# Output projections of a two-layer trunk: first layer's weight sums added by GpSimd, and the second product's operands in the freed input tiles

## The chip, the core and the metric

The kernel runs on one core of a Trainium2 chip. The time is the device time of one execution in microseconds. Engines work side by side: TensorE (PE, with its weight loads as PEld), VectorE (DVE), ScalarE (ACT), GpSimd (POOL), and SyncE (SP), which here issues nearly all DMAs. Each engine works its own instructions off in a fixed order and waits where an operand isn't there. The granted clock (PEclk) is the clock of TensorE as a share of 2.4 GHz; 0.50 is 1.2 GHz.

## The reference

```python
for i in range(DEPTH):                      # two layers, T = 1024 tokens, D = 1024
    hid = _rmsnorm(x, norm_w[i])
    if i % 2 == 0: x = x + _gated_deltanet(hid, ...)   # layer 0
    else:          x = x + _mamba2(hid, ...)           # layer 1
return _rmsnorm(x, final_norm_w)
# each mixer: project hid, convolve, gates, a chunked scan over tokens giving y (T x 2048),
# a gated norm of y, and last the output projection:
#   return y @ w_out                        # (1024 x 2048) times (2048 x 1024), float32
# layer 0, in each chunk of 64 tokens: a unit lower triangular solve with a_mat
```

All in float32. A float32 product is made here of three products of operands split in a high and a low part (hi x hi, hi x lo, lo x hi).

## The kernel before, in words

Both layers have the same course. The normalised hidden rows lie transposed in SBUF in tiles of `apool` (tags a0 to a3, two buffers each of 128 x 4 x 512). Eight groups of heads follow each other. In layer 0, while group g is scanned over its chunks (`scan`), the triangular inverse of group g+1 (`inverse`) and its projections run between, handed out slot by slot in the loop at L909. `inverse` stores nte to a DRAM tile xd (L615), reads it back in another layout into X (L618), writes ones on X's diagonal with a GpSimd memset (L619), and solves row by row on VectorE (L630). The scan carries a state S, written by VectorE (L791, L794) and used by TensorE (L771). A finished chunk is normalised (L820 to L825, two small GpSimd instructions per chunk), turned by TensorE (L66) and stored to DRAM as y, `y0d` or `y1d` (L836).

The output projection (`out_proj`, L346) halves y and w_out in both directions and makes the result in seven products of half size instead of eight. The products' weights are, in order, x00, s1, s2, x01, s3, s4, x11, where x are blocks of w_out and s sums of them: s1 = x10 + x11, s2 = s1 + x00, s3 = x00 + x10, s4 = s2 + x01. Their other operands are blocks of y or differences of such: one running tile Tt of differences for products 1, 2 and 6 (L370, L373), and one difference on GpSimd for product 4 (L365). Products are counted from 0 in this text. Each is 8 k-steps of 12 matmuls 128x512 (4 PSUM banks times three, L387 to L389) and a k-step loads a block of weights (L378) and of y (L357), splits each (`split`: a ScalarE cast at L86, a VectorE subtraction at L87), and goes. Products alternate between PSUM banks ps_proj and ps_pt (even) and ps_tr and ps_sc (odd). The scan uses ps_tr and ps_sc.

The sums lie in DRAM. `weight_sums` (L321) makes them with 44 GpSimd-issued DMAs per layer, 16 copies (L338) and 28 that add to what stands there (L340), of 512 KB; the loops take one per slot during the scan. Product 0 (`early`) runs in the last slots of the last group. Products 1 to 6 (`rest`) begin after the scan: they take a new pool `nrm`, which lies where the scan's pool lay and opens when everything of that has ended. In it are the residual rows `xrow` (L416), Tt, u, and the rings of split operands from product 2 on; product 1 splits into `apool` tiles (`big_ring`, a0 to a3), whose hidden rows are no longer needed. `d0` reads product 0's banks out.

What order the engines get is decided ahead by a scheduler that simulates a timeline; the program's order is its input. DMAs marked `keep_in_program_order` stay in theirs.

## Time and profile before

| | us |
|---|---|
| median of 3 runs (2013.79 to 2020.08) | 2018.72 |
| profiled execution | 2022.02 |
| its span | 2020.3 |
| TensorE busy | 1886.5 |
| VectorE busy | 1402.6 |
| ScalarE busy | 1081.1 |
| GpSimd busy | 576.1 |

The busy times are those of the profiled execution, and the span is that of its instructions. GpSimd's busy time leaves out the DMAs that it issues. TensorE's share is an average over the stages: a hole in it counts in full, and work of the other engines counts only where TensorE waits for it.

### The profile page before, as it was taken

To read this page: it belongs to the slowest core of one execution; us is meant where nothing else is said; L and a number is where in the kernel's file an instruction comes from. 1 tells how busy PE (TensorE), PEld (TensorE's weight loads), DVE (VectorE), ACT (ScalarE), POOL (GpSimd) and SP (SyncE) were. 2 spreads that over 40 slices of the span, in tenths; PEclk is the share of its full clock that TensorE was granted. 3 is DMA by queue.
4 is the path that set the end of the run, shared out by engine and by line. 5 is a ranking of instruction groups with operands and counts; after the bars stand their busy time and mean duration, and the time that the engine had idled before them with its cause. 6 is when DMAs were issued, how large, how long until landed. Compare 5 with 4: busy or idle time off the path is not lost. (4 is left out here: it accounts for less than half of the span.)

```text
span 2020.3 us, 36051 instructions
## 1 busy us (share of the span) xinstructions
PE 1886.5 (93%) x12782; PEld 1615.4 (80%) x12782; DVE 1402.6 (69%) x3011; ACT 1081.1 (54%) x2933; POOL 576.1 (29%) x962
## 2 busy tenths in 40 slices
PE   7996989898998989899799999999999999998897
PEld 5775878787887878788588788888888888887786
DVE  5795767676768676765488777666576666666677
ACT  5634656466565646565444565555445455554343
POOL 1112122223222211110324133424343342432253
PEclk9997999899999989999899999999999999999999
DMA  4444354625444532334566245455464443244864
GB/s 142 112 95 87 88 125 100 128 75 141 94 119 85 115 71 75 86 100 136 186 220 216 80 140 130 111 127 111 123 131 120 115 98 87 83 128 128 266 227 151
DMA packets 260087, 249.98 MB, mean 124 GB/s; under 512 B 67345, under 2 KB 182722, under 8 KB 259906
## 3 DMA queue, kind: packets, MB, share of 16 engines
q1 hardware_dynamic: 240066, 201.54, 34.3%
q0 software_dynamic: 19840, 46.14, 12.1%
q8 instruction: 100, 1.64, 0.3%
q14 instruction: 81, 0.66, 0.1%
HBM read 218.06 MB, written 75.69 MB: 145 GB/s over the span
## 5 line engine op out<-in xcount | busy, mean ns | idle before, releaser
L165 PE MATMUL ps_proj<-hid_h,wh 128*128 128x512 f32 x1024 | 411.8, 402 | 0.8 <-ACT gtmp L268 0.5
L166 PE MATMUL ps_proj<-hid_l,wh 128*128 128x512 f32 x1024 | 405.4, 396 | 0.0
L167 PE MATMUL ps_proj<-hid_h,wl 128*128 128x512 f32 x1024 | 405.1, 396 | 0.0
L227 PE MATMUL ps_proj<-zh,hid_h 128*128 128x256 f32 x1024 | 304.4, 297 | 4.0 <-DVE z L234 2.7
L229 PE MATMUL ps_proj<-zh,hid_l 128*128 128x256 f32 x1024 | 299.6, 293 | 0.0
L228 PE MATMUL ps_proj<-zl,hid_h 128*128 128x256 f32 x1024 | 299.0, 292 | 0.0
L165 PEld LDWEIGHTS ps_proj<-hid_h,wh 128*128 128x128 f32 x1024 | 193.1, 189 | 40.7 <-ACT gtmp L268 0.8
L167 PEld LDWEIGHTS ps_proj<-hid_h,wl 128*128 128x128 f32 x1024 | 192.8, 188 | 40.6
L166 PEld LDWEIGHTS ps_proj<-hid_l,wh 128*128 128x128 f32 x1024 | 193.0, 188 | 36.2
L227 PEld LDWEIGHTS ps_proj<-zh,hid_h 128*128 128x128 f32 x1024 | 200.8, 196 | 8.6 <-DVE z L234 3.3
L228 PEld LDWEIGHTS ps_proj<-zl,hid_h 128*128 128x128 f32 x1024 | 200.4, 196 | 3.0
L229 PEld LDWEIGHTS ps_proj<-zh,hid_l 128*128 128x128 f32 x1024 | 200.1, 195 | 0.4
L204 DVE SCALAR_TENSOR_TENSOR acc<-raw,cw_ssd,acc 128x512 f32<-128x512 f32 x192 | 160.5, 836 | 43.3 <-ACT acc L202 40.0
L204 DVE SCALAR_TENSOR_TENSOR acc<-raw,cw_gdn,acc 128x512 f32<-128x512 f32 x192 | 145.1, 757 | 21.5 <-ACT acc L200 20.2
L317 POOL TENSOR_SCALAR_AFFINE_SELECT gcrow<-gcrow 128x512 f32<-128x512 f32 x128 | 95.4, 754 | 187.3 <-DMA gcrow<-gcr_g 126.4
L821 POOL TENSOR_SCALAR so<-so,cq 128x2 f32<-128x2 f32 x64 | 27.3, 427 | 420.2 <-ACT yn L820 420.2
L87 DVE TENSOR_TENSOR wl<-wr,wh 128x512 fp32r<-128x512 f32 x128 | 89.6, 701 | 79.0 <-ACT wh L86 77.5
L630 DVE TENSOR_TENSOR tm<-Dt,X 128x2 f32<-128x2 f32 (+30 forms) x248 | 86.9, 350 | 75.6 <-POOL X L619 68.0
L184 ACT ACTIVATE th<-acc 128x512 f32<-128x512 f32 x128 | 80.2, 627 | 93.6 <-DVE acc L204 93.4
L86 ACT CAST wh<-wr 128x512 fp32r<-128x512 f32 x128 | 78.8, 617 | 75.9 <-PE ps_proj L166 64.4
L197 ACT COPY raw<-ps_proj 128x512 f32<-128x512 f32 x128 | 74.6, 582 | 77.8 <-PE ps_proj L167 73.6
L1010 ACT ACTIVATE lt<-gcrow,ldt_s 128x128 f32<-128x128 f32 x256 | 82.0, 391 | 40.5 <-POOL t L1015 18.0
(308 smaller groups left out, 4441.8 us busy)
## 6 DMA issues: line engine op xcount, KB each, us to landing
wr<-in_gdn_w_in_dram SPq DMA_DIRECT2D x96, 256.0 KB, 3.1
wr<-in_ssd_w_in_dram SPq DMA_DIRECT2D x96, 256.0 KB, 2.9
wo_gs<-in_gdn_w_out_dram POOLq DMA_DIRECT2D x44, 512.0 KB, 6.4
wo_ss<-in_ssd_w_out_dram POOLq DMA_DIRECT2D x44, 512.0 KB, 6.7
yr<-y0d SPq DMA_DIRECT2D x72, 256.0 KB, 3.6
yr<-y1d SPq DMA_DIRECT2D x72, 256.0 KB, 3.5
gcrow<-gcr_g SPq DMA_DIRECT2D x64, 256.0 KB, 3.7
gcrow<-gcr_s SPq DMA_DIRECT2D x64, 256.0 KB, 4.0
```

What stands on the lines that cost most here:

```text
L87: nc.vector.tensor_tensor(out=lo, in0=src, in1=hi.bitcast(F32), op=ALU.subtract)
L165: nc.tensor.matmul(pt[0:nco], hi[:, j, 0:nco], xh[:, j, :], start=first, stop=False)
L166: nc.tensor.matmul(pt[0:nco], hi[:, j, 0:nco], xl[:, j, :], start=False, stop=False)
L167: nc.tensor.matmul(pt[0:nco], lo[:, j, 0:nco], xh[:, j, :], start=False, stop=last)
L184: nc.scalar.activation(th, src, AF.Tanh, scale=0.5)
L204: nc.vector.scalar_tensor_tensor(out=acc, in0=raw[:, k:k + 512], scalar=cw[:, k * 32 + ti:k * 32 + ti + 1], in1=acc, op0=ALU.mult, op1=ALU ...
L227: nc.tensor.matmul(pt, xh, zh[:, k, :], start=k == 0, stop=False)
L228: nc.tensor.matmul(pt, xh, zl[:, k, :], start=False, stop=False)
L229: nc.tensor.matmul(pt, xl, zh[:, k, :], start=False, stop=k == KT - 1)
L317: nc.gpsimd.affine_select(out=t, in_=t, pattern=[[0, 4], [1, P]], compare_op=ALU.is_ge, fill=-1e30, base=0, channel_multiplier=-1)
L630: nc.vector.tensor_tensor(out=tv, in0=Dt[:, r0:, s:], in1=X[:, s:s + 1, s:].to_broadcast([P, nr, nj]), op=ALU.mult)
L1010: nc.scalar.activation(lt[:, h, :], rows[h][:, n % 4, :], AF.Exp, bias=ldt[:, h0 + h, n:n + 1])
```

## The change

For layer 0 (`made` false) no sums are made in DRAM. Products 1, 2, 4 and 5 load blocks of w_out and GpSimd adds them in SBUF (`w_form`): s1 into tiles W1 (two `apool` tiles a1), on which s2 and s4 go on adding; s3 in place. That is 32 additions 128x512 and 16 more weight loads. In layer 1 the DMAs stay. Product 1's differences go to N1 (two `apool` tiles a0) in both layers, and its split operands to a2 and a3 alone. In layer 0 the differences of products 1 and 4 are made by VectorE, in layer 1 by GpSimd as before. Loading the residual rows and reading out product 0 move behind the third k-step of product 1, two more fetches behind the fifth. Layer 0's allocation of the next hidden tiles moves from product 1 to product 5. The early product's steps are spread 2, 2, 1, 1 over the last slots, one behind the flush, the rest at the end.

```diff
-    def out_proj(yd, forms, resid):
+    def out_proj(yd, X, made, resid):
...
+        N1, W1 = [], []
...
             if i == 4:
                 a, b = load_y(1, 1, j), load_y(0, 1, j, "raw")
-                nc.gpsimd.tensor_tensor(out=a, in0=a, in1=b, op=ALU.subtract)
+                (nc.gpsimd if made else nc.vector).tensor_tensor(out=a, in0=a, in1=b, op=ALU.subtract)
                 return a
-            d = Tt[:, j, :]
             if i == 1:
-                a, b = load_y(0, 0, j), load_y(0, 1, j, "raw")
-                nc.gpsimd.tensor_tensor(out=d, in0=a, in1=b, op=ALU.subtract)
+                a, b, d = load_y(0, 0, j), load_y(0, 1, j, "raw"), N1[j // 4][:, j % 4, :]
+                (nc.gpsimd if made else nc.vector).tensor_tensor(out=d, in0=a, in1=b, op=ALU.subtract)
             else:
-                a = load_y(*{2: (1, 1), 6: (1, 0)}[i], j)
-                nc.vector.scalar_tensor_tensor(out=d, in0=d, scalar=-1.0, in1=a, op0=ALU.mult, op1=ALU.subtract)
+                a, d = load_y(*{2: (1, 1), 6: (1, 0)}[i], j), Tt[:, j, :]
+                nc.vector.scalar_tensor_tensor(out=d, in0=N1[j // 4][:, j % 4, :] if i == 2 else d, scalar=-1.0, in1=a,
+                                               op0=ALU.mult, op1=ALU.subtract)
             return d
 
+        ring_at = [0]
+
+        def load_x(f, j):
+            raw = wring.tile([P, 512], F32, tag=("wr", "wh", "wl")[ring_at[0] % 3], name="wr", bufs=3)
+            ring_at[0] += 1
+            nc.sync.dma_start(raw, X[f][j * P:(j + 1) * P, :])
+            return raw
+
+        def w_form(f, j):
+            if made or f[0] == "x":
+                return load_x(f, j)
+            add = lambda d, a, b: nc.gpsimd.tensor_tensor(out=d, in0=a, in1=b, op=ALU.add)
+            if f == "s3":
+                a, b = load_x("x00", j), load_x("x10", j)
+                add(a, a, b)
+                return a
+            d = W1[j // 4][:, j % 4, :]
+            if f == "s1":
+                add(d, load_x("x10", j), load_x("x11", j))
+            else:
+                add(d, d, load_x({"s2": "x00", "s4": "x01"}[f], j))
+            return d
+
         def pieces(i, j, ring, Tt):
-            raw = wring.tile([P, 512], F32, tag=("wr", "wh", "wl")[j % 3], name="wr", bufs=3)
-            nc.sync.dma_start(raw, forms[wf[i]][j * P:(j + 1) * P, :])
+            raw = w_form(wf[i], j)
...
-        def big_ring(j):
-            a = apool.tile([P, 4, 512], F32R, tag=("a0", "a1", "a2", "a3")[j % 4], name="wy", bufs=2)
-            return [a[:, q, :] for q in range(4)]
+        def in_a(tags):
+            def ring(j):
+                a = apool.tile([P, 4, 512], F32R, tag=tags[j % len(tags)], name="wy", bufs=2)
+                return [a[:, q, :] for q in range(4)]
+            return ring
         banks0 = []
         def early():
             banks0.extend(U())
-            yield from product(0, banks0, big_ring)
+            yield from product(0, banks0, in_a(("a0", "a1", "a2", "a3")))
         def rest(npool, nw, on_rows, before_last=lambda: None):
             rows = {t: [npool.tile([P, D], F32, tag="xr", name="xrow", bufs=NT) for _ in range(4)] for t in range(2)}
             Tt = npool.tile([P, 8, 512], F32, tag="T", name="Tt", bufs=1)
             u = npool.tile([P, 4, 512], F32, tag="u", name="u", bufs=1)
+            N1.extend(apool.tile([P, 4, 512], F32, tag="a0", name="N1", bufs=2) for _ in range(2))
+            if not made:
+                W1.extend(apool.tile([P, 4, 512], F32, tag="a1", name="W1", bufs=2) for _ in range(2))
             half = lambda t, p, c: rows[t][p][:, c * 512:(c + 1) * 512]
             def fetch(t, c):
...
-            fetch(0, 0)
-            for p in range(4):
-                nc.scalar.copy(u[:, p, :], banks0[p])
-                put(0, p, 0, banks0[p], ALU.add)
+            def d0():
+                for p in range(4):
+                    nc.scalar.copy(u[:, p, :], banks0[p])
+                    put(0, p, 0, banks0[p], ALU.add)
...
             for i, done in ((1, d1), (2, d2), (3, d3), (4, d4), (5, d5)):
                 banks = V() if i % 2 else U()
-                for j, _ in enumerate(product(i, banks, big_ring if i == 1 else ring, Tt)):
-                    if j == 3 and i == 1:
+                for j, _ in enumerate(product(i, banks, in_a(("a2", "a3")) if i == 1 else ring, Tt)):
+                    if (i, j) == (1, 2):
+                        fetch(0, 0)
+                        d0()
+                    if (i, j) == (1, 4):
                         fetch(1, 0)
                         fetch(1, 1)
-                    if j == 3 and i == 3:
+                    if (i, j) == (3, 3):
                         fetch(0, 1)
-                if i == 1:
+                if i == 5:
                     before_last()
                 for p in range(4):
                     done(p, banks[p])
...
-    wo0, steps0 = weight_sums(gw_out, "g")
-    early0, rest0 = out_proj(yd0, wo0, lambda n: x[n * P:(n + 1) * P, :])
-    early1, rest1 = out_proj(yd1, wo1, lambda n: x1d[n])
+    wo0 = {f"x{c}{k}": gw_out[k * 1024:(k + 1) * 1024, c * 512:(c + 1) * 512] for c in range(2) for k in range(2)}
+    early0, rest0 = out_proj(yd0, wo0, False, lambda n: x[n * P:(n + 1) * P, :])
+    early1, rest1 = out_proj(yd1, wo1, True, lambda n: x1d[n])
...
             S = scan(g)
             for slot in range(8):
-                next(steps0, None)
                 if g == 7 and slot > 3:
                     next(early0)
-                    next(early0)
+                    if slot < 6:
+                        next(early0)
                 for c in "SIJ":
...
             if g < 6:
                 for _ in k_products(g + 2):
                     pass
+            elif g == 7:
+                next(early0)
             next(S, None)
             if g < 7:
                 z_weights(g + 1)
+        for _ in early0:
+            pass
     hid2 = {}
```

On GpSimd's queue, in layer 0's second inverse: Dt and X are tiles of the solve, `wo_gs` the sums in DRAM. Before:

```order
L623 MEMSET Dt 64x16
L624 MEMSET Dt 64x16
L340 DMA wo_gs_337<-in_gdn_w_out_dram 256x512
L196 COPY raw<-raw 128x3
L340 DMA wo_gs_339<-in_gdn_w_out_dram 256x512
L194 MEMSET raw 128x3
L340 DMA wo_gs_340<-in_gdn_w_out_dram 256x512
L317 AFFINE_SELECT gcrow<-gcrow 128x512 x2
L638 MEMSET Ds 32x16x32
L619 MEMSET X 128x32
```

and after:

```order
L655 MEMSET Dt 64x16
L656 MEMSET Dt 64x16
L196 COPY raw<-raw 128x3
L194 MEMSET raw 128x3
L317 AFFINE_SELECT gcrow<-gcrow 128x512 x2
L651 MEMSET X 128x32
L670 MEMSET Ds 32x16x32
```

The three summing DMAs are gone from before the memset of X, and the memset of Ds has moved behind it.

On TensorE, at the end of layer 0's scan: L808, now L840, is the last matmul of a chunk's output, L66 turns the normalised chunk, L387, now L411, begins three matmuls of the projection. Before:

```order
L806 MATMUL ps_sc<-S,qT 128x256
L808 MATMUL ps_sc<-p,att 128x128 x2
L66 MATMUL ps_tr<-ident,yn 128x128 x5
L387 MATMUL ps_tr<-wy 128x512
L388 MATMUL ps_tr<-wy 128x512
L387 MATMUL ps_tr<-wy 128x512
L388 MATMUL ps_tr<-wy 128x512
L387 MATMUL ps_sc<-wy 128x512
```

and after:

```order
L838 MATMUL ps_sc<-S,qT 128x256
L840 MATMUL ps_sc<-p,att 128x128 x2
L411 MATMUL ps_sc<-wy 128x512
L412 MATMUL ps_sc<-wy 128x512
...
L413 MATMUL ps_sc<-wy 128x512
L66 MATMUL ps_tr<-ident,yn 128x128 x4
L411 MATMUL ps_tr<-wy 128x512
L412 MATMUL ps_tr<-wy 128x512
L413 MATMUL ps_tr<-wy 128x512
```

The matmuls of product 1 on the ps_sc banks (24 of them) now stand ahead of the last four turns, those on the ps_tr banks behind them.

On SP's queue, at the same place: `y0d<-yg` are the stores of y, `nw` and `xrow` the first loads into the new pool, `wr` and `yr` weights and y of the products. Before:

```order
L378 DMA wr<-wo_gs_338 128x512 x2
L836 DMA y0d_331<-yg 128x2x128 x3
L836 DMA y0d_332<-yg 128x2x128 x4
L91 DMA nw<-in_norm_w_dram 128x1024
L416 DMA xrow<-in_x_dram 128x512 x4
L357 DMA yr<-y0d_330 128x512
L357 DMA yr<-y0d_329 128x512
L416 DMA xrow<-in_x_dram 128x512 x8
```

and after:

```order
L359 DMA yr<-y0d_329 128x512 x2
L868 DMA y0d_331<-yg 128x2x128
L383 DMA wr<-in_gdn_w_out_dram 128x512 x2
L359 DMA yr<-y0d_331 128x512
L359 DMA yr<-y0d_329 128x512
L383 DMA wr<-in_gdn_w_out_dram 128x512 x4
L868 DMA y0d_331<-yg 128x2x128 x2
L868 DMA y0d_332<-yg 128x2x128 x4
L91 DMA nw<-in_norm_w_dram 128x1024
L445 DMA xrow<-in_x_dram 128x512 x12
L359 DMA yr<-y0d_331 128x512 x3
```

All of product 1's loads, and the first of product 2's, now stand ahead of the last six stores of y, and all twelve first loads of residual rows follow in one piece.

## Rows read from the trace of the kernel before

**Rows 1.** The page, part 1: busy us, share of the span, instructions.

```profile
PE 1886.5 (93%) x12782; PEld 1615.4 (80%) x12782; DVE 1402.6 (69%) x3011; ACT 1081.1 (54%) x2933; POOL 576.1 (29%) x962
```

**Rows 2.** Waits, VectorE, whole span: line and releaser: total us, times, longest.

```profile
DVE tm L630 <- POOL X L619: 68.0, 7, 18.5
```

**Rows 3.** Waits, TensorE, from 150 to 850 us.

```profile
PE ps_sc L771 <- DVE S L794: 26.7, 8, 5.4
...
PE ps_sc L771 <- DVE S L791: 8.8, 1, 8.8
```

**Rows 4.** Timeline, second and last inverse: start, us, engine, line, what [idle before].

```profile
156.33 2.03 SPq L615 DMA_DIRECT2D xd<-nte  x4
157.04 0.92 POOL L340 DMA_DIRECT2D wo_gs<-in_gdn_w_out_dram  x1 [3.49 <-DMA wo_gs<-in_gdn_w_out_dram]
174.93 0.16 POOL L619 MEMSET X<- 128x32 f32 x1 [10.02 <-DMA X<-xd]
...
817.40 2.08 SPq L615 DMA_DIRECT2D xd<-nte  x4
829.06 0.16 POOL L619 MEMSET X<- 128x32 f32 x1 [0.91 <-DMA X<-xd]
829.25 0.16 DVE L630 TENSOR_TENSOR tm<-Dt,X 128x2 f32<-128x2 f32 x1 [5.87 <-POOL X L619]
```

**Rows 5.** Source line L340: ns min/median/max, first and last start.

```profile
L340 POOL DMA_DIRECT2D wo_gs<-in_gdn_w_out_dram x28: 878/966/1617, 137.5 to 715.2; - x28
```

**Rows 6.** Timeline, TensorE, end of layer 0's scan and product 1.

```profile
975.07 0.61 PE L808 MATMUL ps_sc<-p,att 128*128 128x128 f32 x4
...
988.14 0.79 PE L387 MATMUL ps_tr<-wy 128*128 128x512 f32 x1 [8.23 <-ACT wy L86]
...
993.90 0.49 PE L387 MATMUL ps_tr<-wy 128*128 128x512 f32 x1
```

**Rows 7.** Timeline, GpSimd, same place.

```profile
983.73 4.18 POOL L370 TENSOR_TENSOR Tt<-yr 128x512 f32<-128x512 f32 x3 [5.00 <-issue]
```

**Rows 8.** Timeline, SP, same place.

```profile
955.62 26.28 SPq L836 DMA_DIRECT2D y0d<-yg  x7
```

**Rows 9.** Windows: us, busy PE PEld DVE ACT POOL, PEclk, DMA share, GB/s.

```profile
985.00:1010.00 25.00, 21.75 (x83) 17.32 (x84) 14.28 (x18) 7.78 (x15) 9.41 (x7) 0.82 0.93 337
988.00:992.00 4.00, 3.78 (x8) 2.48 (x8) 3.57 (x7) 1.13 (x3) 0.00 (x0) 0.50 1.03 393
1054.00:1076.00 22.00, 22.00 (x99) 18.22 (x98) 14.38 (x20) 12.17 (x25) 8.91 (x11) 1.00 0.71 241
```

**Rows 10.** Timeline, TensorE, end of layer 1's scan and product 1.

```profile
1861.92 0.22 PE L1040 MATMUL ps_sc<-xs,mt 128*64 128x64 f32 x1
...
1874.60 0.79 PE L387 MATMUL ps_tr<-wy 128*128 128x512 f32 x1 [7.34 <-ACT wy L86]
...
1879.77 0.40 PE L387 MATMUL ps_tr<-wy 128*128 128x512 f32 x1
```

**Rows 11.** Lines by form, VectorE: busy us, mean ns, idle before.

```profile
L87 DVE TENSOR_TENSOR yl<-yr,yh 128x512 fp32r<-128x512 f32 x48 | 48.9, 1019 | 32.8 <-ACT yh L86 30.5 <-PE ps_tr L389 2.3
L87 DVE TENSOR_TENSOR yl<-Tt,yh 128x512 fp32r<-128x512 f32 x32 | 21.8, 682 | 0.0
```

**Rows 12.** Timeline, VectorE, end of layer 0's scan.

```profile
976.38 0.42 DVE L816 TENSOR_TENSOR o<-ps_sc,o 128x256 f32<-128x256 f32 x1 [1.49 <-ACT o L815]
```

**Rows 13.** Source lines L365 and L86: ns min/median/max.

```profile
L365 POOL TENSOR_TENSOR yr<-yr x16: 1291/1430/1852, 1046.1 to 1952.8; 128x512 f32<-128x512 f32 x16
L86 ACT CAST yh<-yr x48: 604/622/627, 1026.7 to 1976.2; 128x512 fp32r<-128x512 f32 x48
```

**Rows 14.** Timeline, SP, end of layer 1's scan.

```profile
1870.28 1.85 SPq L416 DMA_DIRECT2D xrow<-x1d  x4
```

**Rows 15.** DMA issues: count, KB each, median us to landing.

```profile
wr<-in_gdn_w_out_dram SPq DMA_DIRECT2D x24, 256.0 KB, 3.9
xrow<-x1d SPq DMA_DIRECT2D x16, 256.0 KB, 5.4
```

More of the change, by code (lines that the diff above doesn't have):

```diff
@@ L1101, in hybrid_trunk @@
                     next(early1)
-                    next(early1)
+                    if slot < 6:
+                        next(early1)
                 next(S, None)
@@ L1105, in hybrid_trunk @@
             flush()
+            if g == 7:
+                next(early1)
             next(S, None)
+            for _ in early1 if g == 7 else ():
+                pass
             if g < 7:
```

## The prediction

> **What bounds the kernel now.** I read the page's first two parts, then the waits by engine, the source lines that the change touches, and the timeline and the windows at each place where they showed a hole. TensorE is busy for 93% of the span [rows 1], so only its holes and the stretches at half clock can give time. There are three kinds that this change reaches.
>
> First, the scan of layer 0. Between two groups of heads VectorE stands still before its triangular solve, at L630, seven times, 68.0 us together, 18.5 at the longest [rows 2]; it waits for a GpSimd memset of X (L619), which waits for a trip through DRAM: nte is stored to xd (L615) and read back. TensorE then waits at L771 for the state S that VectorE has not written, 26.7 + 8.8 = 35.5 us [rows 3]. In the second group the store is issued at 156.33 and the memset follows at 174.93, 18.6 us later; in the last group 817.40 and 829.06, 11.7 [rows 4]. Between them lies one difference: behind the store at 156.33 GpSimd issues three accumulating DMAs of 512 KB, from 157.04 on, while the 28 of them end at 715.2 [rows 4, 5], so none is left for the last group, whose VectorE wait is 5.87, the shortest.
>
> Second, the first product of layer 0's output projection that starts after the scan (product 1). The last scan matmul ends at 975.7, product 1 starts at 988.14 [rows 6]. It waits for Tt, a tile of a pool that opens when the scan's pool closes: the first GpSimd difference runs at 983.73 and three take 4.18 us [rows 7]; the pool closes behind the last stores of y, which SP issues until about 982 [rows 8]. Product 1 then runs at the lower of the two clock levels: from 988 to 992 the granted clock is 0.50 (1.2 GHz of 2.4) with DMA at 393 GB/s [rows 9]. Third, the same in layer 1: scan over at 1862.1, product 1 at 1874.60, full speed from 1879.77 [rows 10].
>
> **The change part by part.** *Scan of layer 0.* The 44 accumulating DMAs go; nothing else in the seven inverses changes but the order of a few small instructions. If each VectorE wait became the 5.87 of the group without them, 7 x 5.87 = 41.1 would be left of 68.0: 26.9 saved on VectorE. On TensorE 35.5 us stand against these 68.0, so 0.52 of a VectorE microsecond reaches it: 14.0 saved. Bounds: 0, if the group without sums is short because it is the last and lighter, and 26.9, if it arrives one for one, as the half clock behind each stall is repaired too. I take 14.0, from the one ratio that was measured.
>
> *Gap of layer 0.* The differences of product 1 go to N1, in the input tiles a0 that the scan has given back, made by VectorE (8 x 0.68, by VectorE's subtraction of the same shape [rows 11]), and product 1 draws a2 and a3 alone. Nothing of it needs the new pool. It needs the ps_sc banks, which VectorE reads until 976.80 [rows 12]; so it can start there, and 988.14 - 976.80 = 11.3 goes. The half clock goes with it: twelve matmuls took 993.90 - 988.14 = 5.8 us [rows 6], while 99 in 22.00 us, 0.222 each [rows 9], would take 2.7: 3.1 more. Against it stands the tail of the scan, which takes in eight VectorE subtractions, the splits, twelve GpSimd additions and some 28 loads between its last stores. The chain of the last four normalisations sits in these queues; bounds 0 and 5 us (one GpSimd addition of 1.43, as L365 takes [rows 13], ahead of three or four of its small operations). I take 2.
>
> *Products 2 to 6 of layer 0.* TensorE is busy 22.00 of 22 there [rows 9], so the cover is full and any loss shows. The fifth product gets 16 weight loads for 8 beside its 16 loads of y: 32 x 256 KB = 8.4 MB in 96 matmuls x 0.222 = 21.3 us, 394 GB/s, where 241 flow now. At the peak of 393 that costs nothing; at the 337 that a 25 us stretch sustained [rows 9], 24.9 us, 3.6 more; at 241, 34.8, which is 13.5 more. I take 3.0, near the middle one, since loads can run some steps ahead. VectorE takes over eight subtractions, 8 x 0.68 = 5.4 on 14.38 of 22 [rows 9], so about 20 of 22: just covered. GpSimd's 32 additions, 32 x 1.43 = 46 us over the tail and four products, are less than half of their time; the 8 + 8 subtractions that left it pay for half.
>
> Rows show what such additions do to VectorE: its subtraction of the split took 1019 ns beside GpSimd's subtractions (48, of which 16 accompany one) and 682 in the products without them [rows 11]; 48 x 0.337 = 16 us, 1.0 per GpSimd instruction. In the fifth product eight GpSimd additions replace eight GpSimd subtractions, so nothing is added there. The Trainium skill, SBUF — State Buffer, section "Who interferes with whom", says that a VectorE instruction with two inputs in SBUF contends with a GpSimd instruction that reads SBUF, and that the loser blocks for the whole instruction; the rows agree in sign and by about the size of one instruction. By that rule the 32 additions are not free for VectorE, though GpSimd makes them: 32 x 1.0 = 32 us blocked less 16 for the subtractions that leave GpSimd, spread over the tail and four products, 4 us each, which the 7.6 us that VectorE has free in 22 would hold.
>
> For the transfers, the Trainium skill, DMA: Bandwidth & Descriptors, section "Specifications", gives one core about 358 GB/s from HBM. By it the fifth product would need an estimated 23.4 us, 2.1 lost instead of 3.0; the slice at 393 shows that the figure isn't a ceiling here.
>
> Sum for the projection of layer 0: 11.3 + 3.1 - 2.0 - 3.0 = 9.4 saved (bounds 14.4 saved, 4 lost).
>
> *Projection of layer 1.* The same gap goes: 1874.60 - 1862.1 = 12.5, and 5.2 us for twelve matmuls against 2.7, 2.5 more [rows 10]. Four transposes between cost 0.6. The weight sums remain DMAs, the differences remain on GpSimd, but eight of them now stand in its queue among the small operations of the last normalisations: 1.5 by the median of one such instruction [rows 13]. And a new wait is added: the residual rows and the reading out of the first product's banks (d0) are moved behind the third k-step of product 1, and the third product wants those banks after 48 matmuls of product 1, 10.7 us after the scan, at about 1873.4. The rows of x are loaded into the new pool; SP issues them from 1870.28, behind the last stores, and they take 5.4 to land [rows 14, 15]: 1875.7, and 0.68 for the first addition: at least 3.0 of waiting, more as SP's queue holds more loads ahead of them; up to 8. I take 5. Queued behind the waiting matmul on TensorE is the rest of product 1, which needs nothing more: order alone holds it. Saved: 12.5 + 2.5 - 0.6 - 1.5 - 5.0 = 7.9 (bounds 11.4 and 0).
>
> Total 14.0 + 9.4 + 7.9 = 31.3. The profiled execution took 2022.02, 3.3 above the median of 2018.72 and 1.7 above its own span of 2020.3; taken from it 1990.7, at the median **1987**.
>
> **The rivals.** *B: the sums are not what delays xd.* For it: VectorE's first wait, 18.5, is much longer than the rest can explain by three DMAs, and xd is written in rows of 32 numbers whatever runs beside it. Against it: 11.7 without. Then the scan gives nothing: 2018.7 - 17.3 = 2001. *C: the scan gives all.* 26.9, and TensorE's stalls with their half clock: 2018.7 - 26.9 - 17.3 = 1974. For it: TensorE stalls while VectorE does; against: 0.52. *D: layer 0's products become bound by transfers.* Fifth product 13.5 lost, tail 5, gap 14.4 won: 4.1 lost; 14.0 - 4.1 + 7.9 = 17.8, 2001. For it: 394 wanted, 337 sustained; against: it is one product in six. B and D together: 4 us saved, 2015, no change that can be told. *E: slower.* In the 16 k-steps with two weight loads the chain load 3.9, addition 1.43, cast 0.62, subtraction 0.68 = 6.6 [rows 13, 15] isn't covered by the steps loaded ahead, against the 12 x 0.222 = 2.7 that TensorE takes of a step: 16 x 3.9 = 62 lost, 31 net at full price. It decides from half the chain uncovered; at three quarters, 2034. Against it: nine tiles for raw weights hold four steps.
>
> **How the numbers follow.** Forecast 0.54 (own range 1977 to 1997), B 0.16, C 0.12, D 0.06, B with D 0.06, E 0.06. A measurement of this kernel can tell 0.3%, 6 us, from no change. The first four are faster by more, 0.88, less 0.02 for what of B and D lies above 2012.7: 0.86; same 0.08; slower 0.06. The range from 1966 to 2012 takes in C and leaves out E, B with D and the far ends of the terms.
>
> **What would show it.** Waits of VectorE at the solve near 6 us each, some 41 in all, and TensorE's at the state near 21: the scan's step right; unchanged: B. Product 1 of layer 0 within 2 us of the last scan matmul, no slice at 0.50 there. Products 2 to 6 at 22.00 of 22, the fifth with DMA share near 1; a TensorE wait on a weight cast there would be D or E. In layer 1 product 1 right behind the scan, then one wait of about 5 us for the first bank of the third product. I am wrong if the scan's holes have another cause, or if the loads of the tail delay its last stores by more than the gap that goes.

## The result, and the profile after

| | before | after |
|---|---|---|
| median of 4 runs, us | 2018.4 | 2000.45 |
| lowest to highest, us | 2013.79 to 2020.08 | 1990.88 to 2002.65 |
| profiled execution, us | 2022.02 | 1990.88 |

The ratio is 0.990, 95% interval 0.9868 to 0.9932: 18 us faster. The two traces stand 31.1 us apart, because that of before comes from an execution 3.6 above its median and that of after from the lowest of its executions; a second trace of the changed kernel (below) is of one of 2004.16, 3.7 above the median of its set.

Page, parts 1 and 2 of after (columns as in [rows 1]; then the granted clock in 40 slices, 9 being full):

```profile
PE 1886.8 (95%) x12782; PEld 1611.4 (81%) x12782; DVE 1427.4 (72%) x3027; ACT 1078.9 (54%) x2933; POOL 572.7 (29%) x934
...
PEclk9997999999999999999999999999999999999999
```

TensorE's busy time is that of [rows 1] to 0.3 us; 31 us of its holes are gone. One slice, at the second inverse, has a clock of 7 tenths, all others 9. First the scan: the waits of the solve, and TensorE's waits for the state from 150 to 850 us, answering to [rows 2, 3].

```profile
DVE tm L662 <- POOL X L651: 38.9, 7, 11.4
```

```profile
PE ps_sc L803 <- DVE S L826: 5.1, 4, 2.4
PE ps_sc L803 <- DVE S L823: 1.7, 1, 1.7
```

VectorE's seven waits fell from 68.0 to 38.9, 2.2 under the 41.1 of the forecast. They are not seven alike, though: the longest is 11.4, in the second group, and the other six come to 27.5. TensorE's fell from 35.5 to 6.8, by 28.7 and not by 14. The second inverse, answering to [rows 4] (start, us, engine, line, what, idle before):

```profile
155.59 2.16 SPq L647 DMA_DIRECT2D xd<-nte  x4
```

```profile
167.07 0.16 POOL L651 MEMSET X<- 128x32 f32 x1 [8.39 <-PE ps_sc L811]
```

From the store to the memset pass 11.5 us where it was 18.6, and 11.7 in the group that had no sums beside it.

The end of the scan of layer 0 on TensorE and SP, answering to [rows 6, 8], and ScalarE there:

```profile
946.64 0.61 PE L840 MATMUL ps_sc<-p,att 128*128 128x128 f32 x4
947.74 0.50 PE L411 MATMUL ps_sc<-wy 128*128 128x512 f32 x1 [0.49 <-DVE o L848]
...
963.25 0.50 PE L411 MATMUL ps_tr<-wy 128*128 128x512 f32 x1 [2.93 <-ACT wy L86]
```

```profile
946.45 10.89 SPq L868 DMA_DIRECT2D y0d<-yg  x4
960.62 0.34 SPq L91 DMA_DIRECT2D nw<-in_norm_w_dram  x1
```

```profile
960.63 1.07 ACT L475 COPY u<-ps_proj 128x512 f32<-128x512 f32 x2 [1.69 <-DMA y0d<-yg]
961.59 1.09 ACT L475 COPY u<-ps_pt 128x512 f32<-128x512 f32 x2
962.55 0.65 ACT L86 CAST wy<-N 128x512 fp32r<-128x512 f32 x1
```

On VectorE, and the granted clock behind the stop (columns as in [rows 9]):

```profile
960.66 1.90 DVE L374 SCALAR_TENSOR_TENSOR Tt<-N,yr 128x512 f32<-128x512 f32 x3 [6.80 <-DMA y0d<-yg]
...
963.23 0.69 DVE L87 TENSOR_TENSOR wy<-N,wy 128x512 fp32r<-128x512 f32 x1
```

```profile
964.00:966.50 2.50, 2.50 (x8) 1.93 (x7) 0.42 (x1) 2.50 (x6) 1.07 (x1) 0.50 0.91 301
```

Product 1 starts 0.5 us behind the scan. It stops 2.9 us before 963.25, though: its fifth step waits for a cast that stands on ScalarE behind the copies of d0, and these wait for the new pool, which opens when the last y store has landed, at 960.6. On VectorE the subtractions of the same step stand behind three differences into Tt, a tile of that pool too. The wait for the pool has moved from before product 1 into it, and behind the stop the clock is 0.50 once more.

Windows of the fourth and fifth product (columns as in [rows 9]), VectorE's instructions in the fifth (busy us, mean ns, idle before), and a piece of its timeline with GpSimd's additions (L389) beside them:

```profile
999.10:1022.60 23.50, 22.08 (x98) 17.93 (x97) 16.83 (x18) 7.95 (x14) 14.19 (x9) 1.00 0.70 240
1022.60:1051.90 29.30, 24.41 (x97) 18.75 (x96) 26.25 (x28) 12.25 (x26) 20.67 (x16) 0.94 0.89 288
```

```profile
L367 DVE TENSOR_TENSOR yr<-yr 128x512 f32<-128x512 f32 x6 | 8.8, 1469 | 1.4 <-DMA yr<-y0d 1.3
L87 DVE TENSOR_TENSOR yl<-yr,yh 128x512 fp32r<-128x512 f32 x9 | 8.6, 955 | 0.7 <-ACT yh L86 0.7
L87 DVE TENSOR_TENSOR wol<-wr,woh 128x512 fp32r<-128x512 f32 x7 | 6.9, 989 | 0.0
...
L454 DVE TENSOR_TENSOR xrow<-ps_tr,xrow 128x512 f32<-128x512 f32 x2 | 1.4, 677 | 0.0
```

```profile
1023.15 3.37 POOL L389 TENSOR_TENSOR wr<-wr 128x512 f32<-128x512 f32 x2 [4.45 <-DVE yr L367]
1023.59 1.78 DVE L87 TENSOR_TENSOR wol<-wr,woh 128x512 fp32r<-128x512 f32 x1
...
1028.20 1.83 POOL L389 TENSOR_TENSOR W<-W,wr 128x512 f32<-128x512 f32 x1 [1.68 <-DMA wr<-in_gdn_w_out_dram]
1028.20 0.67 DVE L87 TENSOR_TENSOR wol<-wr,woh 128x512 fp32r<-128x512 f32 x1
1028.80 0.68 DVE L454 TENSOR_TENSOR xrow<-ps_tr,xrow 128x512 f32<-128x512 f32 x1
```

The fifth product lasts 29.3 us where it had 21.8. VectorE is busy 26.25 us of them, with its instructions that have both inputs in SBUF stretched to 955 to 1469 ns in the mean, the ones with a PSUM operand not (677 in the mean, 0.68 at 1028.80 beside an addition). Transfers run at 288 GB/s at a share of 0.89. Two things are scarce at once.

Layer 1, end of the scan, on TensorE, and SP, answering to [rows 10, 14]:

```profile
1838.55 0.22 PE L1076 MATMUL ps_sc<-xs,mt 128*64 128x64 f32 x1
1838.84 0.47 PE L411 MATMUL ps_sc<-wy 128*128 128x512 f32 x1
...
1854.65 0.77 PE L411 MATMUL ps_proj<-woh,yh 128*128 128x512 f32 x1 [3.36 <-DMA xrow<-x1d]
```

```profile
1848.40 7.57 SPq L445 DMA_DIRECT2D xrow<-x1d  x12
```

As forecast: product 1 behind the scan, at 1838.84, then one wait of 3.4 for the third product's bank, which is read out only when the residual rows have landed.

### The profile page after: what moved, and what is told of

It reads as the page before. It is cut to its first block, busy times and chain, and to the rows that moved or that the text cites. A ratio compares the mean times of both kernels' runs of the same rounds, so it can differ in the third digit from the quotient of the medians.

```text
span 1989.1 us, 36021 instructions
## 1 busy us (share of the span) xinstructions
PE 1886.8 (95%) x12782; PEld 1611.4 (81%) x12782; DVE 1427.4 (72%) x3027; ACT 1078.9 (54%) x2933; POOL 572.7 (29%) x934
## 3 DMA queue, kind: packets, MB, share of 16 engines
q1 hardware_dynamic: 242370, 205.73, 35.5%
## 4 chain that ended last, share of the span: by engine, by line
PE 34%; DMA 6%; DVE 6%; POOL 2%; issue 2%; ACT 2%; SPq 0%; POOLq 0%; DVEq 0%; ACTq 0%
PE ps_proj L165 5%; PE ps_proj L166 4%; PE ps_proj L167 4%; DMA gcrow<-gcr_s 2%; PE ps_proj L227 2%; PE ps_proj L228 2%; PE ps_proj L229 2%; PE ps_sc L1075 1%; PE ps_tr L66 1%; DVE acc L204 1%; PE ps_proj L412 1%; DMA yr<-y0d 1%; PE ps_proj L413 1%; PE ps_pt L411 1%; PE ps_proj L411 1%
## 5 line engine op out<-in xcount | busy, mean ns | idle before, releaser
L227 PE MATMUL ps_proj<-zh,hid_h 128*128 128x256 f32 x1024 | 300.1, 293 | 2.7 <-DVE z L234 2.7
L227 PEld LDWEIGHTS ps_proj<-zh,hid_h 128*128 128x128 f32 x1024 | 196.7, 192 | 7.6 <-DVE z L234 4.0
L662 DVE TENSOR_TENSOR tm<-Dt,X 128x2 f32<-128x2 f32 (+30 forms) x248 | 86.4, 348 | 46.7 <-POOL X L651 38.9
L86 ACT CAST wh<-wr 128x512 fp32r<-128x512 f32 x128 | 78.7, 616 | 69.9 <-PE ps_proj L166 60.6
```

The lines of the kernel that those rows point to most:

```text
L227: nc.tensor.matmul(pt, xh, zh[:, k, :], start=k == 0, stop=False)
L662: nc.vector.tensor_tensor(out=tv, in0=Dt[:, r0:, s:], in1=X[:, s:s + 1, s:].to_broadcast([P, nr, nj]), op=ALU.mult)
```

## Experiments

Each ratio is to runs of the kernel before on the same chip. Starts of products are read from the timeline, by counting 96 matmuls a product; the last matmuls of product 1 are mixed with the first of product 2, so the border between these two is one of count alone. The code shown is an excerpt of each edit.

**The changed kernel again.** No edit.

> The changed kernel once more, unedited. Its six executions so far lie at 1991 (two) and 1999 to 2003 (four), with a mean granted clock of 0.977 to 0.979 and 0.971 to 0.974. Theory (clock): the instructions run in the same order and the waits are the same within 2 us, but holes that cost one stretch of half clock in one execution cost two in another; then a profile at about 2000 shows 10 us or more of additional half clock. Rival (transfers): the waits themselves differ, by about 9 us in one place, with the clock following.

Measured: median 2002.42, ratio 0.9883 (0.9855 to 0.9912); trace of 2004.16. Solve waits 39.4 for 38.9; the products as before (29.4 for the fifth). The two traces by stretch, up to the last memset of X and from there to product 1, the first two lines the first trace, the last two this one:

```profile
101.00:796.00 695.00, 662.15 (x5258) 581.87 (x5257) 519.98 (x1428) 418.94 (x1274) 130.85 (x256) 0.98 0.29 73
796.00:948.00 152.00, 135.04 (x1009) 119.35 (x1008) 101.06 (x240) 81.86 (x258) 36.97 (x47) 0.94 0.45 138
```

```profile
103.00:802.00 699.00, 663.47 (x5246) 582.43 (x5245) 520.92 (x1428) 417.88 (x1270) 130.37 (x254) 0.97 0.29 72
802.00:959.00 157.00, 138.09 (x1010) 121.66 (x1010) 103.04 (x240) 82.07 (x257) 36.30 (x47) 0.91 0.44 134
```

Of the 9 us more, 1.3 + 3.1 are TensorE busy for longer at a lower granted clock (0.94 to 0.91 in the second stretch), 2.7 + 1.9 are longer holes; TensorE's waits for the state are 9.6 where they were 6.8. Neither theory alone: small holes move, and the clock with them. The kernel before stood higher in this set too (2027.43, not 2018.4), so the two traces differ in more than the execution; but the changed kernel's times in the first set alone lie 11.8 apart. So a single trace of this kernel carries about 10 us of chance.

**The kernel before without layer 0's sums.**

```
-                next(steps0, None)
-    wo0, steps0 = weight_sums(gw_out, "g")
+    wo0 = {plain blocks x00 .. x11}
+    wo0.update(s1=wo0["x10"], s2=wo0["x00"], s3=wo0["x10"], s4=wo0["x01"])
```

> The kernel before with layer 0's 44 summing DMAs left out; the products load the plain blocks x10, x00, x10, x01 in place of the sums, so the weight sums of layer 0 are left out of what is computed. Nothing else changed. Theory: the DMAs are what makes the solve wait; VectorE's waits at L630 fall from 68 to about 40 us and the scan of layer 0 ends some 25 us earlier, the time falls by 15 to 25 us. Rival: they are not; waits near 68, time within 5 us of before.

Measured: 1986.77, before 2027.43, ratio 0.9817 (0.9777 to 0.9857). VectorE's waits at the solve:

```profile
DVE tm L631 <- POOL X L620: 36.3, 7, 9.7
```

The DMAs are the cause, and worth more than expected. Windows from the first to the last memset of X, before and this:

```profile
101.00:829.00 728.00, 668.72 (x5254) 588.26 (x5253) 521.48 (x1427) 418.87 (x1271) 164.85 (x300) 0.95 0.44 101
```

```profile
103.00:798.00 695.00, 661.75 (x5247) 580.83 (x5245) 520.95 (x1430) 417.19 (x1269) 131.14 (x257) 0.98 0.29 73
```

TensorE's holes fall from 728.0 - 668.7 = 59.3 to 33.3, by 26 for 31.7 less of VectorE's waits, and its busy time by 7.0 at a higher clock (0.95 to 0.98): 33 us. TensorE's waits for the state are 7.9 here.

**Freed tiles alone.**

```
-    wo0 = {plain blocks x00 .. x11}
-    early0, rest0 = out_proj(yd0, wo0, False, ...)
+    wo0, steps0 = weight_sums(gw_out, "g")
+    early0, rest0 = out_proj(yd0, wo0, True, ...)
+                next(steps0, None)          # in each slot
```

> The changed kernel with layer 0's sums made by DMAs again and its differences on GpSimd, as in layer 1; what is left of the change is the freed tiles for product 1 and the later reading out of product 0. Theory: the scan ends where it did before (975), both gaps ahead of product 1 go (12 us each) less a wait of about 4 behind it in each, the fifth product is back at 21.8 us: about 18 us faster than before, near the whole change by its medians. Rival: the freed tiles alone give under 10 us because the wait behind product 1 is what the gap turns into.

Measured: 2011.68, ratio 0.9926 (0.9898 to 0.9955): 16 us. Solve waits 67.2, the scan as in the kernel before. In each layer the gap of 12.7 goes and 5 to 6 come back in product 1: 30.8 us in layer 0 (24.9 before), 29.1 in layer 1 (24.2). The fifth product is at 21.8. So of the 25 us between the medians in this set (2027.43 and 2002.42) 16 come with the freed tiles alone. The additions in place of the DMAs add only 9 to that, though the scan gives some 28 (the last memset of X is at 830.4 here and at 802.3 in the trace of 2004.16): the tail of the scan and the fourth and fifth product take back most of it.

**The same DMAs, narrow.**

```
-    def weight_sums(w_out, nm):
+    def weight_sums(w_out, nm, w=512):
-                            src, dst = X(*p[i])[r, :], forms[f][r, :]
+                            src, dst = X(*p[i])[r, 0:w], forms[f][r, 0:w]
+    _, steps0 = weight_sums(gw_out, "g", 8)
+                next(steps0, None)          # in each slot
```

> The changed kernel with 44 summing DMAs added again in the slots where they stood, of the same 256 rows but 8 numbers a row in place of 512 (8 KB each); nothing reads them. Theory (traffic): it is the 512 KB each that delay xd, so the waits of the solve stay near 39 us and the time within 4 us of the changed kernel. Rival (issuing): it is their issue on GpSimd's queue or their descriptors, so the waits go back to 60 or more and the time up by 15 to 25 us.

Measured: 1999.98, ratio 0.9873 (0.9847 to 0.9899), beside 2002.42 without them. VectorE's waits at the solve:

```profile
DVE tm L663 <- POOL X L652: 37.3, 7, 9.8
```

44 DMAs issued at the same places, of 256 rows each, delay nothing when their rows are short. It is the 512 KB of traffic, not the issuing.

**s3 without its addition, without its second load, without both.**

```
-                add(a, a, b)                # first run: both loads stay
```
```
-                a, b = load_x("x00", j), load_x("x10", j)
-                add(a, a, b)
+                a = load_x("x00", j)
+                add(a, a, a)                # second run
```
```
+                return load_x("x00", j)     # third run: neither
```

> The changed kernel with the eight additions of s3 (fifth product of layer 0) left out; both blocks are still loaded and the product uses x00 alone, so s3 is left out of what is computed. In the changed kernel the fourth and fifth products of layer 0 last 23.5 and 29.4 us in place of 21.8. Theory (VectorE blocked): about ten of VectorE's instructions there last 1.78 us in place of 0.68 beside a GpSimd addition; with eight of sixteen additions gone the two products fall to 22 and 24 or less, 6 to 9 us together. Rival (transfers): 32 loads are still made, so the fifth product stays at 28 to 30 us.

> The changed kernel with the second block of s3 not loaded: x00 is added to itself, so x10 is left out of s3; 24 loads in the fifth product as before the change, and all additions. Theory (VectorE blocked): the additions still block VectorE, the fifth product stays above 26 us. Rival (transfers): with 8 of 32 loads gone it falls to 22 to 24 us.

> The changed kernel with neither the second block of s3 loaded nor the addition made (x00 in place of s3, so s3 is left out). Leaving out one of the two gave 27.9 and 28.4 us for the fifth product and 21.8 for the fourth. Theory (two limits together): with both out the fifth product falls to 22 to 24. Rival (s4's additions, or the subtraction on VectorE, hold it): it stays at 27 or more.

Measured: medians 1997.76, 1995.17, 1997.6 (ratios 0.9865, 0.9858, 0.9863; intervals within 0.0026 of them). The fifth product in each, in this order (columns as in [rows 9]):

```profile
1032.10:1060.00 27.90, 23.16 (x98) 17.64 (x97) 24.62 (x29) 11.72 (x24) 14.69 (x13) 1.00 0.88 284
```

```profile
1029.00:1057.40 28.40, 25.08 (x97) 19.88 (x96) 23.96 (x31) 12.32 (x26) 14.27 (x14) 0.88 0.82 260
```

```profile
1038.60:1063.40 24.80, 22.37 (x98) 17.87 (x97) 21.78 (x28) 11.79 (x25) 11.74 (x12) 1.00 0.81 264
```

The fourth product is back at 21.8 in all three. In the fifth (29.4 in the second trace of the changed kernel), taking away either one gives 1 to 1.5 us, both 4.6. So neither theory alone: without the addition the transfers still run at a share of 0.88, without the load VectorE is still busy 24 of 28 us and stretched by the remaining additions (those of s4, made ahead). 3.0 us of the loss remain without both; this remainder was not taken apart. Nor does any run part the rate of the transfers from the ring of raw weight tiles, which holds half as many steps ahead when a step loads two. It is no clean sum: in the first run the sixth product rose to 23.6, in the second the fifth ran at a clock of 0.88, in the third the third product rose to 28.7 from 21.8, and the medians of the three can't be told from each other. The clean case comes below, with s3 by DMAs.

**Additions of s3 and s4 on VectorE.**

```
+            eng = nc.vector if f in ("s3", "s4") else nc.gpsimd
+            add = lambda d, a, b: eng.tensor_tensor(out=d, in0=a, in1=b, op=ALU.add)
```

> The changed kernel with the 16 additions of s3 and s4 on VectorE in place of GpSimd. Theory (VectorE blocked): an addition costs VectorE 0.68 when it makes it itself and about 1.1 when GpSimd makes it beside it, so VectorE has less to do though it has more instructions: fourth and fifth products 22 and 22 to 25, 5 to 9 us faster in all. Rival (VectorE full): VectorE is busy 26.6 of 30 us there, sixteen more instructions of 0.68 make it 11 us longer: as slow as the changed kernel or up to 5 us slower.

Measured: 1997.37, ratio 0.9869 (0.9839 to 0.9900). Fourth, fifth and sixth product 24.5, 25.8, 23.8: 74.1 for 74.7 of the changed kernel. The fifth (columns as in [rows 9]):

```profile
1029.10:1054.90 25.80, 22.95 (x97) 17.71 (x97) 22.26 (x37) 11.17 (x24) 10.27 (x5) 1.00 0.92 298
```

Nine more instructions of VectorE in the fifth product, and its busy time is 4.0 lower: an addition costs VectorE no more when it makes it itself. The gain is small, and the time can't be told from the changed kernel's; that fits transfers that remain (32 loads, share 0.92).

**d0 later.**

```
                     if (i, j) == (1, 2):
                         fetch(0, 0)
+                    if (i, j) == (1, 6):
                         d0()
```

> The changed kernel with the reading out of product 0 (d0) moved from behind the third k-step of product 1 to behind the seventh, in both layers. Theory (queue): in layer 0 TensorE waits 2.9 us at 963 for a cast that stands on ScalarE behind copies into the new pool, and in layer 1 3.4 us for a bank that d0 frees while the rest of product 1 would have been there to do; with d0 later product 1 runs through, products 1 and 2 together end 3 to 6 us sooner in each layer. Rival: the third product then waits the same time for its banks, since nothing is loaded sooner: within 3 us of the changed kernel.

Measured: 2000.44, ratio 0.9872 (0.9850 to 0.9893): no gain. Product 1 is at 29.8, and product 2 at 26.8 in place of 21.8. In layer 1 nothing changed (28.8): the third product waits 3.3 for residual rows. Layer 0, single lines of ScalarE, VectorE and TensorE:

```profile
968.23 0.62 ACT L86 CAST wy<-N 128x512 fp32r<-128x512 f32 x1
970.60 1.90 DVE L374 SCALAR_TENSOR_TENSOR Tt<-N,yr 128x512 f32<-128x512 f32 x3 [7.37 <-DMA y0d<-yg]
973.15 0.77 PE L412 MATMUL ps_tr<-wy 128*128 128x512 f32 x2 [2.54 <-DVE wy L87]
1005.01 0.79 PE L412 MATMUL ps_proj<-wol,yh 128*128 128x512 f32 x1 [3.35 <-DVE wol L87]
```

The cast now runs ahead of the copies, and TensorE stops all the same: the subtraction that it needs next stands on VectorE behind the differences into Tt, which wait for the pool. So the time is the rival's, but not its reason. Both engines hold product 1 behind work for the new pool, and moving d0 frees one of them. The 3.35 us in product 2 are a wait for VectorE as well, not for banks.

**All sums by DMAs, later in each group.**

```
-                next(steps0, None)
+                for _ in range((0, 0, 0, 1, 1, 1, 1, 2)[slot]):
+                    next(steps0, None)
```
(against the run with freed tiles alone)

> All of layer 0's sums by DMAs, as in the kernel before, but handed out in slots 3 to 7 of each group instead of one in every slot, so that in the program they stand behind the start of the inverse; freed tiles for product 1 as in the changed kernel. Theory (the DMAs delay the solve because they are under way when xd is stored and read): most of the solve's waits shrink, from 67 to 40 or 50 us, and with no additions in the projection the time is 1990 or below, at least 10 us faster than with one in every slot (2011.7). Rival: wherever they stand they delay, since 44 transfers of 512 KB fill as much of the DMA engines' time: waits stay at 60 or more, time near 2010.

Measured: 1996.75, ratio 0.9864 (0.9844 to 0.9884); 0.6% under the run with one in every slot. VectorE's waits at the solve:

```profile
DVE tm L662 <- POOL X L651: 42.9, 7, 14.8
```

In its second inverse, single lines of SP and GpSimd:

```profile
156.43 2.11 SPq L647 DMA_DIRECT2D xd<-nte  x4
157.65 1.91 POOL L340 DMA_DIRECT2D wo_gs<-in_gdn_w_out_dram  x2
171.34 0.16 POOL L651 MEMSET X<- 128x32 f32 x1 [4.81 <-DMA X<-xd]
```

Of the 28 us that the DMAs add to the solve's waits (67.2 and 39.4 with and without them) some 4 are left. In the second group three of them still run beside the trip of xd, and it takes 14.9; in the other six it takes 11.0 to 12.5, with at most one beside it. They still cost elsewhere: from the first to the last memset of X it is 709.9 us, for 728.1 with one in every slot and 695 to 700 in the changed kernel. So the time is short of the expected 1990, and level with the changed kernel (0.9883 on the same chip), though here no product of layer 0 but the first is longer than 21.8.

**s3 by DMAs; s1 and s3 by DMAs.**

```
+    wo0, steps0 = weight_sums(gw_out, "g", ("s3",))          # or ("s1", "s3")
+            if made or f[0] == "x" or f == "s3":
+                if slot == 5:                                # or slot in (5, 6)
+                    next(steps0, None)
                                                              # and with s1:
-                add(d, load_x("x10", j), load_x("x11", j))
+                nc.sync.dma_start(d, X[f][j * P:(j + 1) * P, :])
```

> The changed kernel with s3 alone made by DMAs (8 in place of 44, one in slot 5 of each group); s1, s2 and s4 still by GpSimd. The fifth product has 24 loads and no addition of its own. Theory (two limits together, transfers at 290 GB/s and VectorE blocked): fourth and fifth products back to 22 to 23 us each, 7 to 9 us faster than the changed kernel, about 1992. Rival: eight DMAs give the delay back to the scan, or the additions of s4 alone keep the fifth product at 27: within 3 us of the changed kernel.

> As the run with s3 by DMAs, and s1 too (16 DMAs, in slots 5 and 6): product 1 loads s1 straight into W1, so eight GpSimd additions and eight loads leave the tail of layer 0's scan. From the memset of the last X to the last scan step the changed kernel takes 149 to 154 us, the kernel with no additions there 147, the kernel with s3 by DMAs 150. Theory (the tail is slowed by the additions and loads): it comes to 146 or 147 and the time 2 to 5 us under that with s3 alone, 1989 where before is 2024. Rival: the sixteen DMAs delay the solve by as much, or the tail is set by VectorE's subtractions: within 2 us of it.

Measured: 1992.98, ratio 0.9844 (0.9825 to 0.9864), and 1988.54, ratio 0.9830 (0.9805 to 0.9856). The fifth product with s3 alone:

```profile
1028.00:1051.70 23.70, 22.54 (x97) 17.78 (x96) 19.93 (x27) 11.72 (x24) 12.13 (x12) 1.00 0.82 271
```

The third, fourth and sixth are at 21.8: of the 9 us lost there 7.4 are back, with 24 loads and no addition of s3. The solve's waits stay at 38.5 and 40.2, so these few DMAs give nothing of the delay back. From the last memset of X to the last update of the state on TensorE (L811, the scan step of the expectation) it is 150.0 us with s3, 147.0 with s1 too, 148.8 and 153.6 in the two traces of the changed kernel; to the last scan matmul it is 152.4, 150.8, 151.2 and 156.0. Both beat the kernel before and, by the ratios, the changed kernel (0.988 to 0.990) by about half a per cent, which for the second stands just at the edge of the intervals. The two can't be told from each other by their times.

## Why the prediction was right in its sign and wide range, and where it was wrong

The time fell, and by the mechanisms of the forecast: the solve's waits and both gaps. But 2000.45 lies 13 above the 1987 of the sum and outside the forecast's own range, 1977 to 1997; only the wide range, up to 2012, holds it. 18 us were saved by the medians, 25 in the set of the second trace, where 31.3 were forecast. That the time is that of rivals B and D, 2001, is chance. B's mechanism is not what the traces show, and D's is half of it: the projection of layer 0, of which the forecast had 9.4 saved and D 4.1 lost, lost 6.5 us in the first trace and 10.9 in the second, and the scan gave about twice its term in return.

Two traces of after stand beside that of before; us, less is faster:

| stretch | forecast | first trace | second trace |
|---|---|---|---|
| scan of layer 0, to the last memset of X | -14.0 | -33.0 | -26.8 |
| its tail, to the last scan matmul | +2.0 | +4.6 | +9.4 |
| gap ahead of product 1 | -11.3 | -12.0 | -11.9 |
| product 1 | -3.1 | +4.6 | +4.5 |
| fourth and fifth product | +3.0 | +9.3 | +8.9 |
| layer 1, gap and product 1 | -7.9 | -8.2 | -7.9 |
| all | -31.3 | -31.1 | -17.9 |

The rest, +3.6 and +5.9, lies behind the sixth product of layer 0, nearly all up to the end of layer 1's scan, where the change does little. That stretch takes 762.0 us before, 765.1 and 767.4 in these traces, and 761.1 to 766.7 in the other variants of the changed kernel, so most of it is scatter.

*The scan: the mechanism was right, the term mis-sized by half.* The solve's waits came out as worked out. The step that failed is "0.52 of a VectorE microsecond reaches it". 35.5 of 68.0 is what remained of the waits behind 32.5 us of work that TensorE had to do meanwhile. What is taken from the wait is taken from the uncovered end first: 38.9 - 32.5 = 6.4 should remain, and 6.8 did, where the proportion gives 20.3. The other runs agree roughly: freed tiles alone 67.2 left 34.8 (the rule 34.7), later DMAs 42.9 left 12.2 (10.4, the proportion 22.4), no sums 36.3 left 7.9 (3.8, the proportion 19.0). Rival C had this right. On top comes the clock, for which the forecast had no term: TensorE's busy time up to the last memset fell by 6.6 at 0.98 for 0.95 (5.3 in the second trace), its holes by 26.4 (23.8). That 41.1 met the waits so well is luck in part: the second group waits 11.4 without any sums beside it, so the sums are not its one difference from the last.

*Product 1 of layer 0: right that it starts at once, wrong that nothing in it needs the new pool.* The half clock does go at its start, and comes back behind the stop at 963. The step that failed is "Nothing of it needs the new pool": its tiles don't, but its casts and subtractions stand in queues behind work that does. The forecast put a wait for the pool in layer 1 alone, 5.0, and counted none in layer 0; there d0 stands on ScalarE, and the differences into Tt on VectorE, ahead of product 1's own instructions, as the run with d0 later shows, and product 1 came out 7.7 us longer than the forecast. In layer 1 the wait was 3.4.

*The fifth product: mis-sized, 3.0 for 9 with the fourth.* The sentence "eight GpSimd additions replace eight GpSimd subtractions, so nothing is added there" failed: the eight additions of s4, for the next product, are made in the same stretch, so it was sixteen over the two products, five of s3 in the fourth, three of s3 and eight of s4 in the fifth. VectorE came to 26.25 of 29.3 where 20 of 22 was forecast, beside transfers at 288 GB/s. Rival D named half of this.

The row on blocked VectorE instructions was read rightly and used too little. The Trainium skill, SBUF — State Buffer, section "Who interferes with whom", says that a VectorE instruction with two SBUF inputs contends with a reading GpSimd instruction, and one with at most one SBUF input, outside modes that use both ports, does not. The trace agrees: 1469, 989 and 955 ns for the former, 677 for the one that also reads PSUM.

*The tail.* 2.0 forecast within 0 and 5; 4.6 and 9.4 measured. To the last scan matmul it is 151.2 to 156.6 us in the nine traces with the additions of s1 in it, 149.3 to 150.8 in the three without (freed tiles alone, later DMAs, s1 by DMAs), 146.6 before. So some 3 to 4 come without any addition, and the additions with their loads bring the rest, 0.4 to 7, which scatters.

That the sum met the first trace to 0.2 is chance: 19.0 too little for the scan, 16.6 too little for the tail and the products of layer 0, and the 3.6 that no term held. In the second trace, which stands above its median as far as that of before, it is 12.8 too little for the scan against 20.9 too little for the tail and the products of layer 0 and 5.9 of no term. And the offset from trace to median, 3.3, was taken for known; the executions of both kernels scatter by 6 to 13 us on one chip. Rival B is refuted by the run without sums; E had a place right, the fifth product with its two loads a step, but there it cost 7.6, where E gave 62 for all 16 k-steps with two weight loads.

## What to carry to other kernels

A wait that partly shows is a cover and a remainder: take the saving from the remainder first, not in proportion. When an operation moves to an idle engine, count all of its instances that the scheduler can put beside the busy stretch, those made ahead for later work too, and what each costs its neighbours. A product whose tiles are free can still be held by its place in a queue: look at every engine that prepares its operands, not at the first that shows as the releaser. And background transfers cost by where they run: the same 44 cost 28 us of solve waits beside a dependent DRAM round trip, 4 when most were handed out behind it, and nothing when their rows were short.

## What was not expected of the hardware

VectorE instructions of 0.68 us took 1.78 beside a GpSimd addition, 1.10 more, but only those with both inputs in SBUF. Nor all of these: the one at 1028.20, which began together with the addition, kept its 0.67, and the addition took 1.83 where one alone (at 1014.53) took 1.29. One program, with the same order and the same solve waits within 0.5 us, ran in 1990.88 and, in another set, in 2004.16; about half of the difference in layer 0 was TensorE at a lower granted clock (0.91 for 0.94 in the tail of the scan) and the other half holes that were a little longer.
